# Sixteen pairs in all seven products, rows finished as they complete, stores from a second queue

## The chip, the cores and the metric

One core of a Trainium2 chip runs the kernel. The metric is the device time of one execution in microseconds (us); lower is better. The unchanged kernel has three timed runs and one profiled execution. Engines are named as in the profile: PE (TensorE matmul), DVE (VectorE), ACT (ScalarE), POOL (GpSimd), SP (SyncE); SPq is SP's instruction queue, from which the kernel before issues its DMAs.

## The reference

One residual block on 1024 rows of width 1024, in float32: two attention branches, a gated merge, an output projection and a squared-ReLU MLP of inner width 4096. The change lies in the last two steps and in how their results travel:

```python
merged = gate_sb * (y_sb @ w_sb_out[l]) + gate_diff * (y_diff @ w_diff_out[l])
x = x + rms_norm(merged @ w_o[l], g_post_mix[l])

h = rms_norm(x, g_pre_mlp[l])
u = jnp.square(jax.nn.relu(h @ w_up[l]))
x = x + rms_norm(u @ w_down[l], g_post_mlp[l])
```

`rms_norm(y, g)` divides each row by the root of its mean square and multiplies by `g`.

## The kernel before, in words

Every operand of a matmul is a float32 number split in two: `hi` is a rounded cast (ACT, L607) and `lo` the rest (DVE, L608). A product of two blocks is then three matmuls: hi by hi, hi by lo, lo by hi. A scheduler fixes the order of each engine's instructions ahead of time, from the order of the program and from when buffers come free; on the chip each engine runs its list strictly in order and waits on semaphores. The same is true of SP's list of DMAs. Buffers come from pools with few slots: two for raw loads, four `row` buffers, four wide ones (`wide`), sixteen `big`, twenty-four pages for split operands (`page`, `pair_page`).

**Merge (`finish_tile`, L647 to L688).** For each tile t of 128 rows: the product with `w_o` in two halves, their mean squares on ACT (L666, in the helper at L108), the reciprocal root on POOL (`rstd_of`, L114 to L117), scaling and residual on DVE (L670, L671), a store of the new residual to `x2_dram` (L672), a second mean square (L674), a second norm (L676), eight transposes on PE and, for tiles 0 to 6, a store of the transposed tile to `h_dram` (L688). Tile 7 stays on the chip and is put straight into `hraw` (L684). `load_h` (L707) reads the other tiles back as `hraw`. Between tiles the program loads and splits the first four pairs' blocks of `w_up` (`ahead`, L751) and makes the first pair's weight sums on POOL (`sums0`, L754).

**Up projection (`up_pair`, L816).** The inner width is sixteen pairs n. Each pair is done as a 2x2 block product with seven block products in place of eight (84 matmuls a pair). The products `c` of the first four pairs are begun early (L776 to L787): `p` is a copy of the first product (L783), then PE adds the next product to the same bank. A pair leaves u11, u12, u21, u22 after squared ReLU (ACT, L769 and L770). The first fifteen pairs make sums S1 to S4 of these on POOL (L866 to L869, tiles `us`); the parts and sums are stored to `s_dram` by SP (L874), in order: A11, A12, A22, S1 to S4. Pair 15 stores its four parts and makes no sums.

**Down projection (L883 to L972).** Again seven block products, named by their left factor: A11, S1, S2, A22, S3, S4, A12. The left factor is read back from `s_dram` (`load_a`), the right factor comes from `w_down` (`load_b`, the `b_a`, `b_b`, ... tiles in `row` buffers) or from differences T1 to T4 of its blocks made on POOL (`sub`, L910; the tiles `t`). Each product runs over eight blocks pp of two pairs. For every pp PE does 24 matmuls, six for each of four row tiles, all four open at once in four PSUM banks. As pair 15 is left out, the last pp has 12, and a product 180. At the end of each product its four banks are added to or copied into `lower` and `upper` (L951 to L972), on ACT, DVE and POOL; after S3 POOL does twelve of these (L966 to L968).

**Pair 15 and the finish (L975 to L1014).** After the seven products pair 15 is done plainly: for each of eight row tiles twelve matmuls `dn` (L997), two adds (L1003), the mean square (L1008 at L108), the reciprocal root on POOL, a multiplication by `g_post2` (L1010, on POOL for six tiles, on DVE for two), the residual (L1013, two instructions) and two stores to `out`.

Of the kernel before, what the change touches and what calls it, by code (L numbers as in the profile page):

```python
# [16 lines left out]
P = 128  # L17
# [24 lines left out]
def hybrid_block_kernel(  # L42
# [67 lines left out]
    def rstd_of(ms, pool, name):  # L110
# [25 lines left out]
        for name in ("A11", "A12", "A21", "A22", "S1", "S2", "S3", "S4")  # L136
# [510 lines left out]
    def finish_tile(t):  # L647
# [168 lines left out]
    def up_pair(n):  # L816
# [46 lines left out]
        if n < UP - 1:  # L863
            us12, us34 = wide(f"us12_{n}"), wide(f"us34_{n}")
            s1, s2, s3, s4 = us12[:, 0, :], us12[:, 1, :], us34[:, 0, :], us34[:, 1, :]
            nc.gpsimd.tensor_tensor(s1, u12, u22, op=ALU.add)  # L866
            nc.gpsimd.tensor_tensor(s2, s1, u11, op=ALU.subtract)
            nc.gpsimd.tensor_tensor(s3, u11, u12, op=ALU.subtract)
            nc.gpsimd.tensor_tensor(s4, u21, s2, op=ALU.subtract)  # L869
            parts |= {"S1": s1, "S2": s2, "S3": s3, "S4": s4}  # L870
        else:
            parts["A21"] = u12
        for name, part in parts.items():
            nc.sync.dma_start(out=s_dram[name][n // 2][:, n % 2, :], in_=part)  # L874
# [4 lines left out]
    for n in range(UP):  # L879
        up_pair(n)  # L880


    PP = UP // 2  # L883
    wd = w_down.rearrange("(pp e j p) (k d) -> j k pp p e d", e=2, j=2, p=P, k=2)
    lower, upper, p5s, chain = [], [], [], []

    def entries(pp):
        return 2 if pp < PP - 1 else 1

    def load_a(name, pp):  # L890
        raw = raw_tile(f"{name}_{pp}", [P, 2, HALF])
        n = entries(pp)
        nc.sync.dma_start(out=raw[:, :n, :], in_=s_dram[name][pp][:, :n, :])
        return raw

    def load_b(j, k, pp, name):
        raw = row(f"b{j}{k}_{name}_{pp}", [P, 2, HALF])
        n = entries(pp)
        nc.sync.dma_start(out=raw[:, :n, :], in_=wd[j, k, pp, :, :n, :])
        return raw  # L900

    def parts_of(raw, name, pp):
        n = entries(pp)
        hi, lo = pair_page(f"{name}_hi{pp}"), pair_page(f"{name}_lo{pp}")
        split(hi[:, :n, :], lo[:, :n, :], raw[:, :n, :])
        return hi, lo

    def sub(out, in0, in1, pp):
        n = entries(pp)
        nc.gpsimd.tensor_tensor(out[:, :n, :], in0[:, :n, :], in1[:, :n, :], op=ALU.subtract)  # L910

    def right(name, pp):

        if name == "B11":
# [21 lines left out]

    for left, other in zip(STORED, ("B11", "T1", "T2", "T4", "T3", "B22", "B21")):
        accs = [bank(BANKS[t], f"d{left}_{t}") for t in range(4)]
        for pp in range(PP):
            a_hi, a_lo = parts_of(load_a(left, pp), f"l{left}", pp)  # L940
            b_hi, b_lo = parts_of(right(other, pp), f"r{other}", pp)
            for e in range(entries(pp)):
                for t in range(4):
                    ts = slice(t * P, (t + 1) * P)
                    for i, (st, mv) in enumerate(((a_hi, b_hi), (a_hi, b_lo), (a_lo, b_hi))):
                        nc.tensor.matmul(  # L946
                            accs[t], st[:, e, ts], mv[:, e, :],
                            start=(pp == 0 and e == 0 and i == 0), stop=(pp == PP - 1 and i == 2),
                        )
        for t in range(4):  # L950
            if left == "A11":  # L951
                lower.append(big.tile([P, 2, HALF], F32, tag="big", name=f"lower{t}"))
                nc.scalar.copy(lower[t][:, 0, :], accs[t])
            elif left == "S1":
                if t % 2 == 0:
                    p5s.append(big.tile([P, 2, HALF], F32, tag="big", name=f"p5_{t}"))
                nc.scalar.copy(p5s[t // 2][:, t % 2, :], accs[t])
            elif left == "S2":
                nc.vector.tensor_tensor(lower[t][:, 1, :], accs[t], lower[t][:, 0, :], op=ALU.add)
            elif left == "A22":  # L960
                upper.append(big.tile([P, 2, HALF], F32, tag="big", name=f"upper{t}"))
                nc.scalar.copy(upper[t][:, 0, :], accs[t])
            elif left == "S3":
                v, q, p4, p5 = lower[t][:, 1, :], upper[t][:, 1, :], upper[t][:, 0, :], p5s[t // 2][:, t % 2, :]
                nc.vector.tensor_tensor(q, accs[t], v, op=ALU.add)
                nc.gpsimd.tensor_tensor(p4, q, p4, op=ALU.subtract)  # L966
                nc.gpsimd.tensor_tensor(q, q, p5, op=ALU.add)
                nc.gpsimd.tensor_tensor(v, v, p5, op=ALU.add)  # L968
            elif left == "S4":
                nc.vector.tensor_tensor(lower[t][:, 1, :], accs[t], lower[t][:, 1, :], op=ALU.add)  # L970
            else:
                nc.vector.tensor_tensor(lower[t][:, 0, :], accs[t], lower[t][:, 0, :], op=ALU.add)  # L972


    g_post2 = load_row(2, big.tile([P, D], F32, tag="big", name="grow2"))  # L975
    last_a, last_b = [], []
    for j in range(2):
        raw = raw_tile(f"last_a{j}", [P, 2, HALF])
        for i in range(2):
            nc.sync.dma_start(out=raw[:, i, :], in_=s_dram[f"A{i + 1}{j + 1}"][PP - 1][:, 1, :])  # L980
        parts = pair_page(f"last_a_hi{j}"), pair_page(f"last_a_lo{j}")
        split(*parts, raw)
        last_a.append(parts)
        raw = row(f"last_b{j}", [P, 2, HALF])
        f = NF - 2 + j
        nc.sync.dma_start(out=raw, in_=w_down[f * P:(f + 1) * P, :].rearrange("p (k d) -> p k d", k=2))
        parts = pair_page(f"last_b_hi{j}"), pair_page(f"last_b_lo{j}")
        split(*parts, raw)
        last_b.append(parts)
    for i, t in enumerate((4, 5, 6, 7, 0, 1, 2, 3)):  # L990
        c, ts = t // 4, slice((t % 4) * P, (t % 4 + 1) * P)
        accs = [bank(BANKS[(2 * i + n) % 4], f"dn_{t}_{n}") for n in range(2)]
        for j in range(2):
            (a_hi, a_lo), (b_hi, b_lo) = last_a[j], last_b[j]
            for p, (st, mv) in enumerate(((a_hi, b_hi), (a_hi, b_lo), (a_lo, b_hi))):
                for n in range(2):
                    nc.tensor.matmul(  # L997
                        accs[n], st[:, c, ts], mv[:, n, :],
                        start=(j == 0 and p == 0), stop=(j == 1 and p == 2),
                    )  # L1000
        tot = (upper if c else lower)[t % 4]
        for n in range(2):
            nc.vector.tensor_tensor(tot[:, n, :], accs[n], tot[:, n, :], op=ALU.add)  # L1003
        tot = tot.rearrange("p a b -> p (a b)")
        xt, o = row(f"xf_{t}"), row(f"of_{t}")
        nc.sync.dma_start(out=xt, in_=x2_dram[t * P:(t + 1) * P, :])
        s2 = pb.tile([P, 1], F32, tag="ssq1", name=f"sf2_{t}", bufs=4)
        mean_square(tot, o, s2)  # L1008
        r = rstd_of([s2], pb, f"f{t}")
        (nc.vector if i > 5 else nc.gpsimd).tensor_tensor(tot, tot, g_post2, op=ALU.mult)  # L1010
        for n in range(2):
            ns = slice(n * HALF, (n + 1) * HALF)
            nc.vector.scalar_tensor_tensor(o[:, ns], tot[:, ns], r, xt[:, ns], op0=ALU.mult, op1=ALU.add)  # L1013
# [51 lines left out]
```

## Time and profile before

| what | value |
|---|---|
| median of three runs | 1494.95 us (1494.24 to 1495.29) |
| profiled execution, its own time | 1494.08 us |
| its span | 1492.4 us |
| outside the span | 1.68 us |
| PE busy | 1443.9 us, 97% of the span |
| DVE, ACT, POOL busy | 64%, 50%, 28% |
| DMA | 217.88 MB, 146 GB/s on average |

The span runs from the first to the last instruction of the profiled execution. PE's busy time is modelled per matmul with overlap, so the time of a run of matmuls is read from their starts. Where this text says cadence, it means the distance between the starts of two matmuls that follow each other.

### The profile page before, as it was taken

The page shows a single profiled execution, that of the slowest core. Times are in us where ns is not written, and L with a number is a line of the kernel's source. Part 1 is how long each engine was busy: PE and PEld are TensorE (multiplying, and loading weights), DVE is VectorE, ACT ScalarE, POOL GpSimd, SP SyncE. Part 2 cuts the span into 40 slices and gives each one's busy share as a digit, 9 for nine tenths or more (in the row PEclk, how much of TensorE's full clock was granted, in tenths as well). Part 3 has the DMA queues.
Part 4 walks back from the last instruction along what each step waited for, and adds up shares of the span by engine and source line. Part 5 has one row for each costly group of instructions (what it writes and reads, how often), then busy time and mean ns, then how long its engine had stood idle before and what let it go on. Part 6 is the DMA issues. An engine that isn't in the chain of part 4 may idle for free. (4 is left out here: it accounts for less than half of the span.)

```text
span 1492.4 us, 20173 instructions
## 1 busy us (share of the span) xinstructions
PE 1443.9 (97%) x7314; PEld 1224.5 (82%) x7314; DVE 955.7 (64%) x1410; ACT 739.4 (50%) x1338; POOL 414.4 (28%) x378
## 2 busy tenths in 40 slices
PE   7999999999999999999999898999999999999993
PEld 6888998898889888888888676887888888888883
DVE  5487988898688857545644675444445598646536
ACT  6456766676465555743334453444444345344312
POOL 2022322230000000000011247656665463334206
PEclk9999999999999999999999999999999999999997
DMA  5342213222332253644356734444446775677615
GB/s 201 81 126 64 71 43 85 71 61 64 85 89 82 78 170 128 212 137 152 102 193 206 269 113 148 162 145 158 158 153 233 246 241 171 209 246 243 202 43 197
DMA packets 93867, 217.88 MB, mean 146 GB/s; under 512 B 9308, under 2 KB 25928, under 8 KB 93768
## 3 DMA queue, kind: packets, MB, share of 16 engines
q1 hardware_dynamic: 93768, 216.61, 44.8%
q8 instruction: 57, 0.93, 0.3%
q14 instruction: 42, 0.34, 0.1%
HBM read 150.75 MB, written 59.79 MB: 141 GB/s over the span
## 5 line engine op out<-in xcount | busy, mean ns | idle before, releaser
L198 PE MATMUL acc_gate<-h_hi,lo_gate 128*128 128x512 f32 x256 | 101.0, 394 | 0.0
L196 PE MATMUL acc_gate<-h_hi,hi_gate 128*128 128x512 f32 x256 | 100.8, 394 | 0.0
L331 DVE TENSOR_TENSOR_SCAN rest<-rest 128x896 f32<-128x896 f32 (+3 forms) x64 | 87.6, 1373 | 20.7 <-POOL rest L326 20.3
L197 PE MATMUL acc_gate<-h_lo,hi_gate 128*128 128x512 f32 x256 | 100.7, 393 | 0.0
L326 POOL TENSOR_SCALAR_AFFINE_SELECT rest<-rest 128x128 f32<-128x128 f32 x64 | 23.6, 369 | 240.3 <-ACT rest L322 223.6
L608 DVE TENSOR_TENSOR w_lo<-raw_up,w_hi 128x1024 fp32r<-128x1024 f32 x32 | 44.4, 1397 | 49.8 <-ACT w_hi L607 43.3
L608 DVE TENSOR_TENSOR lS_lo<-raw_S,lS_hi 128x1024 fp32r<-128x1024 f32 (+1 forms) x32 | 49.3, 1540 | 37.4 <-ACT lS_hi L607 37.3
L607 ACT CAST lS_hi<-raw_S 128x1024 fp32r<-128x1024 f32 (+1 forms) x32 | 32.0, 1000 | 80.8 <-DMA raw_S<-s_dramS 46.8
L116 POOL TENSOR_SCALAR rstd_o<-s 128x1 f32<-128x1 f32 x8 | 2.8, 356 | 244.7 <-DVE or L670 212.8
L946 PE MATMUL dS<-rT_hi,lS_hi 128*128 128x512 f32 x180 | 70.0, 389 | 0.0
L946 PE MATMUL dS<-rT_lo,lS_hi 128*128 128x512 f32 x180 | 70.0, 389 | 0.0
L946 PE MATMUL dS<-rT_hi,lS_lo 128*128 128x512 f32 x180 | 70.0, 389 | 0.0
L567 PE MATMUL mix<-y,hi_mix 128*128 128x512 f32 x256 | 68.6, 389 | 0.0
L394 ACT ACTIVATE s<-s,low 128x896 f32<-128x896 f32 (+7 forms) x64 | 49.7, 777 | 28.3 <-DVE low L389 28.0
L375 POOL MEMSET bias<- 64x64 f32 x4 | 0.6, 144 | 214.0 <-DMA bias<-bias_rows 154.1
L389 DVE CUSTOM_DVE_ANT_0 s<-z,bias 128x512 f32<-128x512 f32 (+3 forms) x64 | 37.0, 586 | 32.0 <-PE z L263 26.7
L608 DVE TENSOR_TENSOR lA_lo<-raw_A,lA_hi 128x1024 fp32r<-128x1024 f32 (+1 forms) x24 | 38.2, 1593 | 28.7 <-ACT lA_hi L607 24.7
L763 PE MATMUL c<-hB_hi,wa_hi 128*128 128x512 f32 x128 | 51.0, 398 | 5.5 <-ACT p L783 5.5
L567 PEld LDWEIGHTS mix<-y,hi_mix 128*128 128x128 f32 x256 | 48.0, 188 | 9.9
L198 PEld LDWEIGHTS acc_gate<-h_hi,lo_gate 128*128 128x128 f32 x256 | 48.1, 188 | 9.2
L197 PEld LDWEIGHTS acc_gate<-h_lo,hi_gate 128*128 128x128 f32 x256 | 48.2, 188 | 8.8
L196 PEld LDWEIGHTS acc_gate<-h_hi,hi_gate 128*128 128x128 f32 x256 | 48.2, 188 | 8.6
(352 smaller groups left out, 4860.7 us busy)
## 6 DMA issues: line engine op xcount, KB each, us to landing
raw_up<-in_w_up_dram SPq DMA_DIRECT2D x32, 512.0 KB, 4.2
s_dramS<-us SPq DMA_DIRECT2D x60, 256.0 KB, 2.4
raw_S<-s_dramS SPq DMA_DIRECT2D x28, 512.0 KB, 4.2
s_dramA<-u SPq DMA_DIRECT2D x49, 256.0 KB, 2.7
raw_A<-s_dramA SPq DMA_DIRECT2D x21, 512.0 KB, 3.7
raw_gate<-in_w_in_dram SPq DMA_DIRECT2D x16, 512.0 KB, 3.7
gate_dram<-gt SPq DMA_DIRECT2D x32, 256.0 KB, 2.5
y<-y_dram SPq DMA_DIRECT2D x16, 512.0 KB, 6.6
```

The costliest lines, as they stand in the source:

```text
L196: nc.tensor.matmul(acc, w_hi[:, ks], h_hi[k][:, cs], start=(k == 0), stop=False)
L197: nc.tensor.matmul(acc, w_hi[:, ks], h_lo[k][:, cs], start=False, stop=False)
L198: nc.tensor.matmul(acc, w_lo[:, ks], h_hi[k][:, cs], start=False, stop=(k == NK - 1))
L326: nc.gpsimd.affine_select(tl[:, dg], tl[:, dg], pattern=[[-1, P]], compare_op=ALU.is_gt, fill=fill, base=0, channel_multiplier=1,)
L331: nc.vector.tensor_tensor_scan(back, back, back, 1.0, op0=ALU.mult, op1=ALU.bypass)
L389: nc.vector.tensor_tensor_reduce(out=s[:, c0:c1], in0=z, in1=bias[:, S - nk + c0:S - nk + c1], scale=1.0, scalar=BIG if prev is None else ...
L394: e = nc.scalar.activation(s[:, :nk], s[:, :nk], AF.Exp, bias=low, scale=-1.0, accum_out=sums[:, m:m + 1],)
L567: nc.tensor.matmul(accs[i][c], st[:, ks], mv[:, cs], start=(first and k % 4 == 0), stop=(last and k % 4 == 3),)
L607: nc.scalar.copy(hi, raw)
L608: nc.vector.tensor_tensor(lo, raw, f32(hi), op=ALU.subtract)
L763: nc.tensor.matmul(acc, st[:, ks], mv, start=(first and k == 0 and i == 0), stop=(k == 3 and i == 2), skip_group_check=True,)
L946: nc.tensor.matmul(accs[t], st[:, e, ts], mv[:, e, :], start=(pp == 0 and e == 0 and i == 0), stop=(pp == PP - 1 and i == 2),)
```

## The change

- All sixteen pairs go through the seven products. `up_pair` makes S1 to S4 for pair 15 too; `A21` is no longer stored, `entries` and the plain `dn` stage are gone. A product has 192 matmuls.
- Rows are finished when their last product is: tiles 4 to 7 after S3; of tiles 0 to 3 the second half's mean square and gain after S4, the first half and the rest after A12. The mean square is taken by halves, the gain is applied by DVE in halves of 512, and `rstd_of` adds two sums. The last four pp of A12 (`BY_TILE`) are done row tile by row tile, so that the tiles end one after the other.
- ACT issues the stores to `x2_dram` (after the mean square), to `h_dram`, and those of A11, A12 and A22. SP keeps S1 to S4, the output and all loads.
- The `ahead` weights are loaded and split after tile 0, not tile 3; `sums0` comes after tile 4, not tile 5; the first two B11 blocks of `w_down` (`first_b`) are loaded ahead of pair 15.

```diff
-        nc.sync.dma_start(out=x2_dram[t * P:(t + 1) * P, :], in_=xt)
         ssq = pb.tile([P, 1], F32, tag="ssq1", name=f"sx_{t}", bufs=4)
         mean_square(xt, o, ssq)
+        nc.scalar.dma_start(out=x2_dram[t * P:(t + 1) * P, :], in_=xt)
...
-            nc.sync.dma_start(out=h_dram[j][c][:, :, ts], in_=ht.rearrange("p (k t) -> p k t", k=4))
+            nc.scalar.dma_start(out=h_dram[j][c][:, :, ts], in_=ht.rearrange("p (k t) -> p k t", k=4))
...
         finish_tile(t)
+        if t == 0:
+            for n in range(AHEAD):
+                first_a.append(split_f0(n, raw_up(2 * n, f"ahead{n}")))
...
-            for n in range(AHEAD):
-                first_a.append(split_f0(n, raw_up(2 * n, f"ahead{n}")))
-        if t == 5:
+        if t == 4:
             sums0 = sums(0, stream.tile([P, HALF], F32, tag="tmp", name="s1_0", bufs=1))
...
-        if n < UP - 1:
...
+        parts |= {"S1": s1, "S2": s2, "S3": s3, "S4": s4}
         for name, part in parts.items():
-            nc.sync.dma_start(out=s_dram[name][n // 2][:, n % 2, :], in_=part)
+            queue = nc.sync if name[0] == "S" else nc.scalar
+            queue.dma_start(out=s_dram[name][n // 2][:, n % 2, :], in_=part)
...
-            b11, b12 = load_b(0, 0, pp, "a"), load_b(0, 1, pp, "a")
+            b11, b12 = first_b[pp] if pp < 2 else load_b(0, 0, pp, "a"), load_b(0, 1, pp, "a")
...
+    for n in range(UP - 1):
+        up_pair(n)
+    first_b = [load_b(0, 0, pp, "a") for pp in range(2)]
+    up_pair(UP - 1)
...
+    def begin_rows(t, tot):
+        xt, o = big_f32(f"xf_{t}"), big_f32(f"of_{t}")
+        nc.sync.dma_start(out=xt.rearrange("p a b -> p (a b)"), in_=x2_dram[t * P:(t + 1) * P, :])
+        s2 = pb.tile([P, 2], F32, tag="ssq", name=f"sf2_{t}", bufs=4)
+        pending[t] = tot, xt, o, s2
+
+    def half_rows(t, n):
+
+        tot, xt, o, s2 = pending[t]
+        mean_square(tot[:, n, :], o[:, n, :], s2[:, n:n + 1])
+        nc.vector.tensor_tensor(tot[:, n, :], tot[:, n, :], g_post2[:, n * HALF:(n + 1) * HALF], op=ALU.mult)
+
+    def end_rows(t):
+        tot, xt, o, s2 = pending[t]
+        r = rstd_of([s2[:, 0:1], s2[:, 1:2]], pb, f"f{t}")
+        for n in range(2):
+            nc.vector.scalar_tensor_tensor(o[:, n, :], tot[:, n, :], r, xt[:, n, :], op0=ALU.mult, op1=ALU.add)
+            nc.sync.dma_start(out=out[t * P:(t + 1) * P, n * HALF:(n + 1) * HALF], in_=o[:, n, :])
...
+            begin_rows(4 + t, upper[t])
+            for n in range(2):
+                half_rows(4 + t, n)
+            end_rows(4 + t)
...
+            half_rows(t, 0)
+            end_rows(t)
...
+        together = PP - BY_TILE if left == "A12" else PP
+        kept = []
         for pp in range(PP):
...
+            factors = parts_of(load_a(left, pp), f"l{left}", pp), parts_of(right(other, pp), f"r{other}", pp)
+            if pp >= together:
+                kept.append(factors)
+                continue
+            for t in range(4):
+                accumulate(accs[t], factors, t, pp == 0, pp == PP - 1)
         for t in range(4):
+            for i, factors in enumerate(kept):
+                accumulate(accs[t], factors, t, False, i == len(kept) - 1)
+            evict(left, t, accs[t])
```

The scheduler puts the new instructions into the engines' lists. The following pieces show three places; the numbers behind the names are buffer numbers.

POOL at the passage from the up to the down projection, before (`us` are the sums S1 to S4, `t` the differences of blocks of `w_down`):

```order
L866 TENSOR_TENSOR us_14_11142<-u_14_11035,u_14_11036 128x512
L868 TENSOR_TENSOR us_14_11143<-u_14_11035 128x512
L867 TENSOR_TENSOR us_14_11142<-us_14_11142,u_14_11035 128x512
L869 TENSOR_TENSOR us_14_11143<-u_14_11036,us_14_11142 128x512
L910 TENSOR_TENSOR t_0_11304<-b_a_11302,b_a_11300 128x1024
L910 TENSOR_TENSOR t_1_11344<-b_a_11342,b_a_11340 128x1024
```

The same place in the change:

```order
L869 TENSOR_TENSOR us_14_11135<-u_14_11028,us_14_11134 128x512
L866 TENSOR_TENSOR us_15_11282<-u_15_11175,u_15_11176 128x512
L868 TENSOR_TENSOR us_15_11283<-u_15_11175 128x512
L867 TENSOR_TENSOR us_15_11282<-us_15_11282,u_15_11175 128x512
L869 TENSOR_TENSOR us_15_11283<-u_15_11176,us_15_11282 128x512
L900 TENSOR_TENSOR t_0_11309<-b_a_11307,b_a_11147 128x1024
L900 TENSOR_TENSOR t_1_11347<-b_a_11345,b_a_11149 128x1024
```

Pair 15's four sums now stand ahead of the first difference `t_0`.

SP at the same passage, before (`b_a` are the loads of `w_down` for the first product; 11380 and 11382 belong to pp 2):

```order
L874 DMA s_dramS_155<-us_14_11143 128x512
L893 DMA raw_A_4_11454<-s_dramA_96 128x1024
L874 DMA s_dramA_123<-u_15_11180 128x512
L874 DMA s_dramA_99<-u_15_11179 128x512
L899 DMA b_a_11380<-in_w_down_dram 128x2x512
L899 DMA b_a_11382<-in_w_down_dram 128x2x512
```

In the change (11383 and 11385 belong to pp 2):

```order
L873 DMA s_dramS_147<-us_14_11135 128x512
L886 DMA raw_A_4_11457<-s_dramA_96 128x1024
L873 DMA s_dramS_123<-us_15_11282 128x512
L873 DMA s_dramS_139<-us_15_11283 128x512
L873 DMA s_dramS_131<-us_15_11282 128x512
L873 DMA s_dramS_147<-us_15_11283 128x512
L891 DMA b_a_11383<-in_w_down_dram 128x2x512
L891 DMA b_a_11385<-in_w_down_dram 128x2x512
```

The loads for pp 2 now stand behind the four stores of pair 15's sums; before, two stores of pair 15's parts stood there.

ACT where the merge ends and the first products `c` of the up projection begin, before:

```order
L687 COPY ht_1_8830<-trh_1_8825 128x512
L108 ACTIVATE or_8900,s_7_8902<-o_0_8833 128x512
L108 ACTIVATE or_8900,s_7_8902<-o_1_8834 128x512
L783 COPY p_0_8932<-c_0_8936 128x512
L108 ACTIVATE or_8900,sx_8912<-xr_8899 128x1024
L783 COPY p_0_8932<-c_1_8937 128x512
```

In the change:

```order
L687 COPY ht_1_8822<-trh_1_8817 128x512
L108 ACTIVATE or_8892,s_7_8894<-o_0_8825 128x512
L108 ACTIVATE or_8892,s_7_8894<-o_1_8826 128x512
L688 DMA h_dram_89<-ht_0_8814 512x1x128
L688 DMA h_dram_91<-ht_1_8822 512x1x128
L108 ACTIVATE or_8892,sx_8903<-xr_8891 128x1024
L674 DMA x_dram<-xr_8891 128x1024
L784 COPY p_0_8924<-c_0_8928 128x512
L784 COPY p_0_8924<-c_1_8929 128x512
```

The two stores of the transposed tile 6 and the store of tile 7's residual stand in ACT's list, and both copies `p` stand behind tile 7's second mean square, where before one of them stood ahead of it.

## Rows read from the trace of the kernel before

**Rows 1.** The page, part 1: busy time and share of the span by engine.
```profile
PE 1443.9 (97%) x7314; PEld 1224.5 (82%) x7314; DVE 955.7 (64%) x1410; ACT 739.4 (50%) x1338; POOL 414.4 (28%) x378
```

**Rows 2.** The chain of waits: start us, length us, what, number of instructions.
```profile
849.54 5.29 PE c L763 x12
...
1203.12 81.60 PE dS L946 x360
...
1447.92 7.95 PE dn L997 x35
```

**Rows 3.** Timeline of the end: start, length, engine, line, operation, [idle before <- releaser].
```profile
1469.07 0.61 PE L997 MATMUL dn<-last_b_hi,last_a_lo 128*128 128x512 f32 x2
...
1487.87 1.42 DVE L1013 SCALAR_TENSOR_TENSOR of<-lower,rstd_f,xf 128x512 f32<-128x512 f32 x2 [0.76 <-POOL rstd_f L117]
```

**Rows 4.** Windows: stretch, length; busy of PE, PEld, DVE, ACT, POOL; PEclk; DMA share; GB/s.
```profile
840.00:860.00 20.00, 14.51 (x58) 11.54 (x58) 13.46 (x17) 8.25 (x17) 7.35 (x8) 0.83 0.65 218
...
1460.00:1480.00 20.00, 9.68 (x43) 7.70 (x41) 11.96 (x19) 4.60 (x8) 13.29 (x13) 0.81 0.76 244
1480.00:1492.00 12.00, 0.00 (x0) 0.00 (x0) 6.60 (x8) 2.30 (x4) 4.51 (x6) 0.50 0.56 206
```

**Rows 5.** Timeline, merge: two half stores of `h_dram`, and one tile's norm by halves.
```profile
785.22 1.20 SPq L688 DMA_DIRECT2D h_dram<-ht  x2
...
787.41 0.59 ACT L108 ACTIVATE or<-o 128x512 f32<-128x512 f32 x1
...
789.18 1.28 DVE L671 SCALAR_TENSOR_TENSOR xr<-or,rstd_o,xr 128x1024 f32<-128x1024 f32 x1 [0.34 <-POOL rstd_o L117]
```

**Rows 6.** Timeline, passage from up to down: loads and casts of pp 2, pair 15's ends.
```profile
1159.23 1.97 SPq L899 DMA_DIRECT2D b_a<-in_w_down_dram  x4
...
1162.19 0.69 DVE L856 TENSOR_TENSOR u<-p_av,v 128x512 f32<-128x512 f32 x1 [5.93 <-issue]
...
1162.61 0.39 PE L763 MATMUL p_tr<-hT_hi,w_lo 128*128 128x512 f32 x1
...
1162.95 1.05 ACT L607 CAST rB_hi<-b_a 128x1024 fp32r<-128x1024 f32 x1 [4.16 <-DMA b_a<-in_w_down_dram]
1163.04 0.69 DVE L859 TENSOR_TENSOR u<-p_tr,v 128x512 f32<-128x512 f32 x1 [0.16 <-PE p_tr L763]
...
1163.90 0.63 ACT L769 ACTIVATE u<-u 128x512 f32<-128x512 f32 x1
...
1173.04 0.39 PE L946 MATMUL dA<-rB_hi,lA_hi 128*128 128x512 f32 x1
```

**Rows 7.** Timeline, same passage: POOL instructions and DVE splits beside them and alone.
```profile
1148.05 1.31 POOL L868 TENSOR_TENSOR us<-u 128x512 f32<-128x512 f32 x1
...
1168.25 1.23 DVE L608 TENSOR_TENSOR rB_lo<-b_a,rB_hi 128x1024 fp32r<-128x1024 f32 x1 [1.52 <-ACT rB_hi L607]
...
1169.32 2.41 POOL L910 TENSOR_TENSOR t<-b_a,b_a 128x1024 f32<-128x1024 f32 x1 [9.03 <-DMA s_dramA<-u]
1169.73 3.08 DVE L608 TENSOR_TENSOR lA_lo<-raw_A,lA_hi 128x1024 fp32r<-128x1024 f32 x1 [0.25 <-ACT lA_hi L607]
```

**Rows 8.** Groups by line, 1180 to 1445 us, POOL: busy, mean ns, idle before.
```profile
L910 POOL TENSOR_TENSOR b_c<-t,b_c 128x1024 f32<-128x1024 f32 (+1 forms) x8 | 22.1, 2763 | 33.3 <-DMA b_c<-in_w_down_dram 33.2
...
L966 POOL TENSOR_TENSOR upper<-upper 128x512 f32<-128x512 f32 x4 | 8.4, 2110 | 24.4 <-DVE upper L965 24.4
L967 POOL TENSOR_TENSOR upper<-upper,p 128x512 f32<-128x512 f32 x4 | 8.0, 2034 | 0.0
L968 POOL TENSOR_TENSOR lower<-lower,p 128x512 f32<-128x512 f32 x4 | 7.7, 1914 | 0.0
```

**Rows 9.** Timeline where the merge ends: DVE's residual of tile 7, PE's next `c`.
```profile
845.56 2.27 DVE L671 SCALAR_TENSOR_TENSOR xr<-or,rstd_o,xr 128x1024 f32<-128x1024 f32 x1 [7.75 <-POOL rstd_o L117]
...
849.54 0.80 PE L763 MATMUL c<-hB_hi,wa_hi 128*128 128x512 f32 x1 [5.49 <-ACT p L783]
```

**Rows 10.** Waits of SP's DMA queue: us in total, times, longest.
```profile
SPq L874 <- ACT u L770: 130.4, 43, 9.4
```

More of the change, by code (lines that the diff above doesn't have):

```diff
@@ L135, in hybrid_block_kernel @@
         name: [dram.tile([P, 2, HALF], F32, name=f"s_dram{name}{i}") for i in range(NF // 4)]
-        for name in ("A11", "A12", "A21", "A22", "S1", "S2", "S3", "S4")
+        for name in ("A11", "A12", "A22", "S1", "S2", "S3", "S4")
     }
@@ L862, in up_pair @@
         parts = {"A11": u11, "A12": u21, "A22": u22}
-        if n < UP - 1:
[L864 to L872, printed above, removed]
+        us12, us34 = wide(f"us12_{n}"), wide(f"us34_{n}")
+        s1, s2, s3, s4 = us12[:, 0, :], us12[:, 1, :], us34[:, 0, :], us34[:, 1, :]
+        nc.gpsimd.tensor_tensor(s1, u12, u22, op=ALU.add)
+        nc.gpsimd.tensor_tensor(s2, s1, u11, op=ALU.subtract)
+        nc.gpsimd.tensor_tensor(s3, u11, u12, op=ALU.subtract)
+        nc.gpsimd.tensor_tensor(s4, u21, s2, op=ALU.subtract)
+        parts |= {"S1": s1, "S2": s2, "S3": s3, "S4": s4}
         for name, part in parts.items():
-            nc.sync.dma_start(out=s_dram[name][n // 2][:, n % 2, :], in_=part)
+            queue = nc.sync if name[0] == "S" else nc.scalar
+            queue.dma_start(out=s_dram[name][n // 2][:, n % 2, :], in_=part)
     def tmp1(name):
         return stream.tile([P, HALF], F32, tag="tmp", name=name, bufs=1)
-    for n in range(UP):
-        up_pair(n)
     PP = UP // 2
+    BY_TILE = 4
     wd = w_down.rearrange("(pp e j p) (k d) -> j k pp p e d", e=2, j=2, p=P, k=2)
     lower, upper, p5s, chain = [], [], [], []
-    def entries(pp):
-        return 2 if pp < PP - 1 else 1
     def load_a(name, pp):
         raw = raw_tile(f"{name}_{pp}", [P, 2, HALF])
-        n = entries(pp)
-        nc.sync.dma_start(out=raw[:, :n, :], in_=s_dram[name][pp][:, :n, :])
+        nc.sync.dma_start(out=raw, in_=s_dram[name][pp])
         return raw
@@ L922, in right @@
         if name == "T2":
-            sub(chain[pp], load_b(1, 1, pp, "b"), chain[pp], pp)
+            sub(chain[pp], load_b(1, 1, pp, "b"), chain[pp])
             return chain[pp]
@@ L926, in right @@
             b21 = load_b(1, 0, pp, "c")
-            sub(b21, chain[pp], b21, pp)
+            sub(b21, chain[pp], b21)
             return b21
@@ L930, in right @@
             b22, b12 = load_b(1, 1, pp, "d"), load_b(0, 1, pp, "d")
-            sub(b12, b22, b12, pp)
+            sub(b12, b22, b12)
             return b12
@@ L935, in right, with accumulate @@
         return load_b(1, 0, pp, "f")
+    def accumulate(acc, factors, t, first, last):
+        (a_hi, a_lo), (b_hi, b_lo) = factors
+        ts = slice(t * P, (t + 1) * P)
+        for e in range(2):
+            for i, (st, mv) in enumerate(((a_hi, b_hi), (a_hi, b_lo), (a_lo, b_hi))):
+                nc.tensor.matmul(
+                    acc, st[:, e, ts], mv[:, e, :], start=(first and e == 0 and i == 0), stop=(last and e == 1 and i == 2)
+                )
+    for n in range(UP - 1):
+        up_pair(n)
@@ new lines, in end_rows, with evict @@
+    def end_rows(t):
[4 more added lines that the diff above has]
+            nc.sync.dma_start(out=out[t * P:(t + 1) * P, n * HALF:(n + 1) * HALF], in_=o[:, n, :])
+    def evict(left, t, acc):
+        if left == "A11":
+            lower.append(big_f32(f"lower{t}"))
+            nc.scalar.copy(lower[t][:, 0, :], acc)
+        elif left == "S1":
+            if t % 2 == 0:
+                p5s.append(big_f32(f"p5_{t}"))
+            nc.scalar.copy(p5s[t // 2][:, t % 2, :], acc)
+        elif left == "S2":
+            nc.vector.tensor_tensor(lower[t][:, 1, :], acc, lower[t][:, 0, :], op=ALU.add)
+        elif left == "A22":
+            upper.append(big_f32(f"upper{t}"))
+            nc.scalar.copy(upper[t][:, 0, :], acc)
+        elif left == "S3":
+            v, q, p4, p5 = lower[t][:, 1, :], upper[t][:, 1, :], upper[t][:, 0, :], p5s[t // 2][:, t % 2, :]
+            nc.vector.tensor_tensor(q, acc, v, op=ALU.add)
+            nc.gpsimd.tensor_tensor(p4, q, p4, op=ALU.subtract)
+            nc.gpsimd.tensor_tensor(q, q, p5, op=ALU.add)
+            nc.gpsimd.tensor_tensor(v, v, p5, op=ALU.add)
+            begin_rows(4 + t, upper[t])
+            for n in range(2):
+                half_rows(4 + t, n)
+            end_rows(4 + t)
+        elif left == "S4":
+            nc.vector.tensor_tensor(lower[t][:, 1, :], acc, lower[t][:, 1, :], op=ALU.add)
+            begin_rows(t, lower[t])
+            half_rows(t, 1)
+        else:
+            nc.vector.tensor_tensor(lower[t][:, 0, :], acc, lower[t][:, 0, :], op=ALU.add)
+            half_rows(t, 0)
+            end_rows(t)
@@ L937, in hybrid_block_kernel @@
     for left, other in zip(STORED, ("B11", "T1", "T2", "T4", "T3", "B22", "B21")):
         accs = [bank(BANKS[t], f"d{left}_{t}") for t in range(4)]
+        together = PP - BY_TILE if left == "A12" else PP
+        kept = []
         for pp in range(PP):
[L940 to L949, printed above, removed]
@@ L950, in hybrid_block_kernel @@
-        for t in range(4):
[L951 to L972, printed above, removed]
@@ L975, in hybrid_block_kernel @@
[L975 to L989, printed above, removed]
@@ L990, in hybrid_block_kernel @@
[L990 to L1013, printed above, removed]
-            nc.sync.dma_start(out=out[t * P:(t + 1) * P, ns], in_=o[:, ns])
```

19 lines of the change are left out of this document (10 added, 9 removed).

## The prediction

> **What bounds the kernel now.** The page's first part comes first: PE is busy 97% of the span [rows 1], so the question is where PE stands still, and what it is given to do. The chain of waits says the same: from 1163 us on it is PE alone, 360 matmuls in 81.60 us [rows 2], a cadence of 226.7 ns, 2.72 us for 12. The reader should see that no load and no split is on the chain there. The windows show two holes. From 1480 us PE does nothing to the end, and in 840 to 860 it is busy 14.51 of 20 us, at a mean granted clock of 0.83 [rows 4]. The end is read from its timeline: the row at 1469.07 holds two `dn` matmuls, so the last starts at about 1469.3; DVE's last two instructions run from 1487.87 to 1489.29 and the span ends at 1492.4 [rows 3]. That is a tail of 23.1 us in which rows queue up behind POOL's norms and gains.
>
> **The sum,** against the profiled execution's own 1494.08 us.
>
> 1. *Matmuls.* Before, 7 x 180 + 96 = 1356; now 7 x 192 = 1344. Twelve fewer at 226.7 ns: **-2.7 us**, all on the chain.
>
> 2. *The tail.* Rows 4 to 7 are done while S4 and A12 still run, and A12's row tiles end 24 matmuls apart, 5.44 us. After the last matmul one row tile is left, of which one half is new: from the last matmul's start to DVE's add 0.43 us (the last `p_tr` at 1162.61, the add L859 at 1163.04 [rows 6]); the add 0.69 [rows 6]; a start of 0.1; from the start of the half's mean square on ACT through the accumulator read and both POOL instructions to DVE's next instruction 1.77 (787.41 to 789.18 [rows 5]), in which DVE's gain for the half, about as long as the add, is hidden; both residual instructions 1.42, and 3.1 from their end to the end of the span [rows 3]. Sum 7.5 us. The tiles do not queue: add, norm and residual are 4 us, less than the 5.44 between tiles. 7.5 in place of 23.1: **-15.6 us.**
>
> 3. *The passage to the down projection.* Here the change adds a wait. Before, the four `b_a` loads of pp 2 and 3 left SP from 1159.23 and pp 2's cast began at 1162.95, 3.72 us later; PE came to pp 2 at 1173.04 [rows 6], so there were ten microseconds in hand. Now POOL has pair 15's four sums ahead of `t_0`, `t_0` must free a `row` buffer before pp 2 can be loaded, and SP has the four stores of those sums ahead of that load. Step by step: u12 is added at 1162.19 to 1162.88 [rows 6]; two ACT instructions of 0.63 [rows 6] give it squared at 1164.2; four POOL sums at 1.31 [rows 7], 1169.5; `t_0` 2.41 [rows 7], 1171.9; issue and landing 3.72 [rows 6], 1175.7; the cast 1.05 [rows 6], 1176.8; the split's `lo`, which the second matmul needs, 1.23 alone or 3.08 beside a POOL difference [rows 7], so 1178.0 to 1179.9. The second matmul was due at 1173.3: PE waits 4.7 to 6.6 us. I take 5.6, the middle, because POOL's `t_2` becomes ready within a microsecond of that split and either may go first. **+5.6 us.** Later pp don't add to it: POOL needs 2.41 per difference, PE 5.44 per pp.
>
>    The row at 1169.73 shows DVE's split at 3.08 us beside POOL's difference, and 1.23 alone [rows 7]. The Trainium skill, page "SBUF — State Buffer", section "SBUF: two separate sides", has a rule for such a pair: a DVE instruction with both inputs in SBUF and a GpSimd instruction that reads SBUF exclude each other for a whole instruction. By that rule the split would wait out `t_2` and the wait would be 6.6, making the sum one microsecond worse; the rows agree with the rule where they overlap, but don't say which of the two starts first.
>
> 4. *The clock after that wait.* After PE's idle 5.49 us at 849.54 [rows 9], the next 12 matmuls took 5.29 in place of 2.72 [rows 2], at half the usual rate, and the window's granted clock was 0.83 [rows 4]; of the two levels 1.2 and 2.4 GHz that is the lower one for a while. A wait of about the same length should cost the same: **+2.6 us**; bounds 0 and 2.6.
>
> 5. *The end of the merge.* Before, PE lost 5.5 us because ACT's second copy `p` stood behind tile 7's second mean square, which waited for DVE's residual at 845.56, 7.75 us late [rows 9]. Now both copies stand behind it, so PE runs dry 12 matmuls earlier, 2.7 us; against that the `ahead` casts and splits no longer sit between tiles 4 and 7, and their loads don't share the queues with those of `sums0`. But `sums0`, one tile earlier, stands ahead of tile 6's norm on POOL and waits for its loads, and ACT has the stores of `h_dram` in its list, which `hraw` waits for. I find terms of up to 4 us in both directions and none that stands out: **0**, bounds -4 and +4.
>
> 6. *Stores from ACT.* SP waited 130.4 us in 43 pieces for ACT's squares before it could store them [rows 10], with loads queued behind. Now 70 stores are issued by ACT. Before shows no DMA issued by ACT; on SP the two `h_dram` stores took 1.20 us together [rows 5], so at most 0.6 each, some 40 us in all, of which ACT, busy 50% [rows 1], hides most. Where it is wanted is the merge, and that price is within point 5. From 860 to 1160 PE is paced by POOL or itself, so neither price nor gain: 0, with -2 as the bound of a gain. The rows would let one expect much more from freeing SP. The Trainium skill, page "DMA: Bandwidth & Descriptors", section "Issuing engines are not separate DMA queues", speaks against that: transfers started from several engines share the same 16 DMA engines, and only issue time is saved. By it no transfer gets shorter and this point stays 0; no row of before can test it.
>
> 7. *The finish of rows 4 to 7.* POOL's twelve instructions after S3 are as before, 24.1 us [rows 8], and the norm of row 4 now stands behind them. DVE, in order, waits there for about 26 us after S3's end, with the split of S4's last pp and of A12's first behind. S4's last pp is due 7 x 5.44 = 38 us after S3's end, A12's first 43.5; DVE gets to them at about 28 and 34. Covered by some 9 us: **0.** SP's loads for A12's third pp stand behind rows 4 to 6 in the same way, due at 54.
>
> Sum: -2.7 - 15.6 + 5.6 + 2.6 = -10.1, so 1484.0 for the profiled execution; it ran 0.87 below the median of the runs, hence **1484.9 us**.
>
> **The rivals.**
>
> *The passage costs nothing (chance 0.17).* If the scheduler's waits let pp 2's load go before `t_0` is done, or pair 15's squares come sooner, points 3 and 4 drop out: 1484.9 - 8.2 = 1476.7. For it: PE has ten microseconds in hand there. Against: POOL's list has nothing else to do first.
>
> *The merge gains (0.12) or loses (0.13)* its 4 us: 1481 or 1489. For a loss: both `p` copies behind the late mean square. For a gain: DMA and ACT are freed of the `ahead` weights where tile 6 was late.
>
> *Slower: DVE starves the tail products (0.04).* One mechanism: POOL's twelve instructions and DVE's splits take turns, DVE waits for row 4's norm, and A12's first split comes after A12 is due. Its price is nothing until the norm is 9 us late; that takes POOL instructions of 2.8 us instead of 2.0. At 4.2 each, 50 us in all, A12 would stand 17 us and lose 2.6 more at the low clock: 1484.9 + 20 = 1505. From about 3.5 us each it is slower than before. Against: the same twelve took 1.9 to 2.1 beside splits in before, and even twice as wide ones take 2.8 [rows 8].
>
> *The tail is not shortened (0.04).* If a row tile's finish waited for another engine, say the x2 load or POOL, each end would take over 5.44 us and pile up to ten more: about 1494, the same as before.
>
> The forecast has the remaining 0.5.
>
> **How the numbers follow.** Between forecast and rivals the bounds are: below, no wait at the passage and a gain of 2, 1475; above, a wait of 6.6, the clock's 2.6 and the merge's 4 with ACT's issues, 1491. Range **1475 to 1491**; some 0.1 lies on either side. A measurement of this kernel can tell about 0.2%, 3 us, from no change. Faster by more than that: forecast, first two rivals: 0.91. Within: the unshortened tail and part of the merge's loss: 0.05. Slower: 0.04.
>
> **What would show it.** Right: no `dn` rows; PE idle once at about 1173 for 5 to 6 us before the 49th `dA` matmul, put down to ACT's cast or DVE's `lo` of `b_a`, with a dozen matmuls at twice the cadence after it; the last matmul about 7.5 us before the span's end; PE without idle from S1 to the end. The merge's step is wrong if PE's loss in 840 to 930 differs by over 4 us. The forecast as a whole is wrong if PE idles in S4 or A12, or if the tail after the last matmul is over 10 us.

## The result, and the profile after

The change takes the median from 1494.6 us (four runs of the kernel before on that chip) to 1483.11 us (1482.16 to 1485.69): a ratio of 0.993, 95% interval 0.9911 to 0.9948. The forecast was 1484.9. The profiled execution ran 1482.92 us; its span went from 1492.4 to 1481.2.

First the chain of waits after the change, the passage to the down projection and the products (start us, length us, what):

```profile
1169.68 2.41 POOL t L900
...
1172.10 3.89 DMA b_a<-in_w_down_dram
...
1176.02 1.05 ACT rB_hi L607
...
1177.11 35.30 PE dA L935 x144
1212.42 87.04 PE dS L935 x384
...
1430.02 43.53 PE dA L935 x192
```

These rows answer to [rows 2]. 384 matmuls take 87.04 us, the cadence of before, 226.7 ns, and `dn` is gone. At the passage the chain leaves PE for POOL's `t`, a load and a cast, as it didn't before. The 144 matmuls behind it take 35.30 us in place of 32.64 (144 at 226.7 ns): 2.7 us at a lower clock, granted at 0.50 in 1176 to 1182 us.

The passage in its timeline, POOL, SP, ACT and DVE, then PE's first matmuls of pp 2:

```profile
1164.57 1.29 POOL L866 TENSOR_TENSOR us<-u,u 128x512 f32<-128x512 f32 x1 [11.68 <-ACT u L771]
...
1165.89 4.18 SPq L873 DMA_DIRECT2D s_dramS<-us  x4
...
1168.43 1.29 POOL L869 TENSOR_TENSOR us<-u,us 128x512 f32<-128x512 f32 x1
...
1172.10 3.21 SPq L891 DMA_DIRECT2D b_a<-in_w_down_dram  x4
...
1177.09 1.23 DVE L608 TENSOR_TENSOR rB_lo<-b_a,rB_hi 128x1024 fp32r<-128x1024 f32 x1 [13.14 <-ACT rB_hi L607]
...
1177.49 3.06 POOL L900 TENSOR_TENSOR t<-b_a,b_a 128x1024 f32<-128x1024 f32 x1 [3.09 <-DMA b_a<-in_w_down_dram]
```

```profile
1177.11 2.08 PE L935 MATMUL dA<-rB_hi,lA_hi 128*128 128x512 f32 x4 [3.69 <-ACT rB_hi L607]
```

The reader sees the steps of the forecast in order, each within 0.4 us of the time worked out for it, and PE idle for 3.69 us. The load leaves at 1172.10, just as `t` (1169.68, 2.41 long) has ended; the four stores of the sums are out two microseconds earlier. Before, the cast for pp 2 stood at 1162.95 [rows 6].

The end, in the timeline of PE and of the others:

```profile
1473.15 0.39 PE L935 MATMUL dA<-rB_hi,lA_lo 128*128 128x512 f32 x1
```

```profile
1473.57 0.69 DVE L995 TENSOR_TENSOR lower<-dA,lower 128x512 f32<-128x512 f32 x1 [1.00 <-PE dA L935]
1474.30 0.63 ACT L108 ACTIVATE of<-lower 128x512 f32<-128x512 f32 x1 [4.71 <-DVE lower L995]
...
1475.05 0.69 DVE L958 TENSOR_TENSOR lower<-lower,grow 128x512 f32<-128x512 f32 x1 [0.79 <-ACT of L108]
1475.12 0.79 POOL L116 TENSOR_SCALAR rstd_f<-sf 128x1 f32<-128x1 f32 x1 [4.00 <-ACT of L108]
...
1476.59 1.41 DVE L964 SCALAR_TENSOR_TENSOR of<-lower,rstd_f,xf 128x512 f32<-128x512 f32 x2 [0.84 <-POOL rstd_f L117]
```

One row tile's chain is all that is left: 8.05 us from the last matmul's start to the span's end at 1481.2, where [rows 3] had 23.1.

PE's waits from 830 to 1165 us (us in total, times, longest):

```profile
PE c L764 <- ACT u L770: 4.1, 2, 2.5
PE p_sc L764 <- ACT w_hi L607: 3.9, 3, 1.6
PE p_sc L764 <- DVE w_lo L608: 2.2, 3, 1.0
PE c L764 <- DVE or L670: 2.2, 1, 2.2
PE p_av L764 <- DVE u L852: 1.8, 1, 1.8
PE c L764 <- ACT p L846: 1.3, 1, 1.3
```

The 5.49 us wait for the copy `p` [rows 9] is gone, and smaller ones have come: for DVE's scaling of tile 7 (L670), for ACT's squares of the first `u` (L770), for copies in the up stage. PE does the merge's last matmul at 833.1 us (835.5 before) and the up stage's last at 1162.8 (1162.6 before). Of these 2.4 us, 0.7 lie ahead of the merge, where the kernels are the same, and 1.7 in the merge; all of it is lost again in the up stage.

So the 11.2 us of span are: 2.7 for twelve matmuls, 15.1 for the tail, less 6.4 for the passage and its clock, less 0.2 up to there. That is one profiled execution of each kernel.

### The profile page after: what moved, and what is told of

Read it like the earlier page. It is cut to its first block, busy times and chain, and to the rows that moved or that the text cites. A ratio compares the mean times of both kernels' runs of the same rounds, so it can differ in the third digit from the quotient of the medians.

```text
span 1481.2 us, 20077 instructions
## 1 busy us (share of the span) xinstructions
PE 1442.6 (97%) x7302; PEld 1222.0 (83%) x7302; DVE 959.9 (65%) x1404; ACT 742.8 (50%) x1350; POOL 406.4 (27%) x376
## 4 chain that ended last, share of the span: by engine, by line
PE 80%; issue 7%; POOL 5%; DVE 3%; DMA 2%; ACT 1%; SPq 0%; POOLq 0%; DVEq 0%; ACTq 0%
PE dS L935 12%; PE dA L935 8%; PE o L656 6%; PE mix L567 6%; PE acc_gate L198 4%; PE acc_gate L196 4%; PE acc_gate L197 4%; PE c L764 3%; PE p_av L764 3%; PE p_tr L764 3%; PE z L263 2%; PE z L262 2%; PE tr_sb L281 2%; PE p_sc L764 1%; PE tr_df L281 1%
## 5 line engine op out<-in xcount | busy, mean ns | idle before, releaser
L608 DVE TENSOR_TENSOR lS_lo<-raw_S,lS_hi 128x1024 fp32r<-128x1024 f32 x32 | 59.7, 1866 | 38.5 <-ACT lS_hi L607 38.3
L935 PE MATMUL dS<-rT_hi,lS_hi 128*128 128x512 f32 x192 | 74.7, 389 | 0.0
L935 PE MATMUL dS<-rT_lo,lS_hi 128*128 128x512 f32 x192 | 74.7, 389 | 0.0
L935 PE MATMUL dS<-rT_hi,lS_lo 128*128 128x512 f32 x192 | 74.7, 389 | 0.0
L607 ACT CAST lS_hi<-raw_S 128x1024 fp32r<-128x1024 f32 x32 | 33.7, 1052 | 78.5 <-DMA raw_S<-s_dramS 50.0
L116 POOL TENSOR_SCALAR rstd_o<-s 128x1 f32<-128x1 f32 x8 | 2.4, 299 | 239.7 <-DVE wa_lo L608 212.2
L726 POOL TENSOR_TENSOR s<-raw_up 128x512 f32<-128x512 f32 x16 | 24.4, 1527 | 117.2 <-DMA raw_up<-in_w_up_dram 87.5
L770 ACT ACTIVATE u<-u 128x512 f32<-128x512 f32 x48 | 29.6, 628 | 51.9 <-DVE u L852 24.5
```

The costliest lines, as they stand in the source:

```text
L608: nc.vector.tensor_tensor(lo, raw, f32(hi), op=ALU.subtract)
L935: nc.tensor.matmul(acc, st[:, e, ts], mv[:, e, :], start=(first and e == 0 and i == 0), stop=(last and e == 1 and i == 2))
```

## The experiments

All are edits of the changed kernel. Ratios are to the kernel before on the same chip. Four chips were used, on which its median was 1493.91 to 1494.10 us, so the medians are compared directly.

| run | median us | ratio, 95% interval |
|---|---|---|
| the changed kernel again | 1484.79 | 0.9944 (0.9932 to 0.9956) |
| sums late | 1479.12 | 0.9901 (0.9887 to 0.9916) |
| all stores on SP | 1479.52 | 0.9901 (0.9889 to 0.9914) |
| weights late | 1481.93 | 0.9919 (0.9906 to 0.9932) |
| stores on SP and weights late | 1483.46 | 0.9933 (0.992 to 0.9945) |
| rows on SP, parts on ACT | 1481.15 | 0.9912 (0.9898 to 0.9925) |
| parts on SP, rows on ACT | 1484.75 | 0.9929 (0.9917 to 0.9941) |
| sums late, all stores on SP | 1472.61 | 0.9855 (0.984 to 0.987) |
| sums late, only parts on ACT | 1476.69 | 0.988 (0.9867 to 0.9894) |
| sums late, only rows on ACT | 1477.76 | 0.9887 (0.9871 to 0.9903) |
| A12 not by tile | 1488.27 | 0.996 (0.9946 to 0.9974) |
| gain of rows 4 to 7 on POOL | 1485.43 | 0.9943 (0.9928 to 0.9958) |

**The yardstick.** The changed kernel without an edit.

> The changed kernel once more, on the same chip as the three others, as their yardstick. Both theories: 1483 us, within 2 us.

1484.79 us, in line. It shows how far one profiled execution can be trusted: the work ahead of the merge, the same in all these kernels, did its last matmul between 740.3 and 742.8 us. The yardstick's own profiled execution took 1488.16 us, and its up projection, from the merge's last matmul to the up stage's last, took 333.4 us, where it had taken 329.8 in the first profile of the same kernel.

**The passage.** Pair 15's sums behind `t_0` and `t_1`, in other buffers:

```diff
+        if n == UP - 1:
+            store(n, parts)
+            late.append((u11, u12, u21, u22))
+        else:
+            store(n, parts | sums_of(n, u11, u12, u21, u22, wide))
...
+    LATE_AT = 1
...
+            if left == "A11" and pp == LATE_AT:
+                store(UP - 1, sums_of(UP - 1, *late[0], pair_f32))
```

> Pair 15's four sums are put behind the first two differences t_0 and t_1 on POOL, and their stores behind the loads of pp 2 and 3 on SP; they live in pages, so that t_0 and t_1 can have the wide buffers of pair 14. Nothing else moves. Theory (the passage wait comes from t_0 and the pp 2 load standing behind the sums): the wait of 3.7 us and the dozen matmuls at the lower clock (2.7 us more) both go, PE runs 384 + 192 matmuls in one piece from 1163 us, and the time falls by 6.4 us to about 1476.7. Rival (the wait only moves: t_2 now stands behind the sums, and pp 4 is late): PE idles at about 1184 in place of 1173 and the gain is under 3 us.

1479.12 us, 5.7 less than the yardstick. In its chain of waits the first product runs through at full rate, and no wait comes in its place:

```profile
1165.60 42.84 PE dA L947 x189
1208.44 87.04 PE dS L947 x384
```

From the up stage's last matmul to the very last it takes 304.0 us, the changed kernel 310.3: the 6.4 us forecast for this run. The cause of the wait is settled, and so is that the slow dozen came with it. The run moves the sums and their stores together; that the load waited for POOL, not for the stores, is read from the timeline above.

**Who issues the stores.** All back on SP:

```diff
-        nc.scalar.dma_start(out=x2_dram[t * P:(t + 1) * P, :], in_=xt)
+        nc.sync.dma_start(out=x2_dram[t * P:(t + 1) * P, :], in_=xt)
-            nc.scalar.dma_start(out=h_dram[j][c][:, :, ts], in_=ht.rearrange("p (k t) -> p k t", k=4))
+            nc.sync.dma_start(out=h_dram[j][c][:, :, ts], in_=ht.rearrange("p (k t) -> p k t", k=4))
-            queue = nc.sync if name[0] == "S" else nc.scalar
+            queue = nc.sync
```

> All stores go back to SP's queue; x2_dram's stays behind the mean square in the program. Theory (who issues the stores is worth nothing, since PE in the up stage waits for POOL and for itself): 1483 within 2 us. Rival (SP's 130 us of waits for ACT's squares held loads back, and freeing SP is a part of the gain): 3 us or more slower than the changed kernel, PE waits in 860 to 1160 us grown by that.

1479.52 us: both theories fell. Stores on SP are neither the same nor slower, but 3.6 to 5.3 us faster than the changed kernel's (1483.11 and 1484.79). Why SP gained nothing from losing them is read from its waits; no run moves the stores of S1 to S4 as well. After the change, over the whole span:

```profile
SPq L873 <- POOL us L866: 128.2, 16, 12.1
```

Before it waited 130.4 us for ACT's squares [rows 10]. The sums S1 to S4 are still in its list, and the first of them waits for POOL, which waits for the same squares. The place of the wait moved by one instruction; the loads behind it gained nothing. POOL's wait for the loads of `w_up`, 880 to 1165 us, stayed too: 82.9 us in 13 pieces before, and after the change

```profile
POOL s L726 <- DMA raw_up<-in_w_up_dram: 86.9, 13, 9.0
```

**The weights.** `ahead` after tile 3 and `sums0` after tile 5 again, once with ACT's stores and once with SP's:

```diff
-        if t == 0:
-            for n in range(AHEAD):
-                first_a.append(split_f0(n, raw_up(2 * n, f"ahead{n}")))
...
+            for n in range(AHEAD):
+                first_a.append(split_f0(n, raw_up(2 * n, f"ahead{n}")))
-        if t == 4:
+        if t == 5:
```

> The ahead weights are loaded after tile 3 again and the first sums after tile 5; all else as in the change. Theory (the merge's gains and losses cancel, PE enters the down projection 0.2 us later than before the change): 1483 within 3 us. Rival (the earlier weights gain several us which the ACT-issued stores give back): 1486 or more, with PE idle in 840 to 860 us as long as before the change or longer.

> Stores on SP and the weights at their former places: of the change, sixteen pairs and the new finish are left, with the early first_b. Theory (the early weights bring PE out of the merge 2 us sooner, and this is kept where SP issues the stores): 2 us above the run with all stores on SP, 1481 to 1482. Rival (early weights are worth nothing or harm, as the run with late weights at 1481.9 beside 1484.8 says): 1479.5 or less.

1481.93 and 1483.46 us. With SP's stores the early weights gain 3.9 us (1483.46 to 1479.52); with ACT's they gain nothing (1481.93 late; 1483.11 and 1484.79 early). The first is as its theory had it, the second 1.5 us above its theory and not near its rival. The profiles put a part of the gain in the merge: from its first matmul to its last it takes 92.2 us in nine of the eleven profiles with early weights, and 94.7 with SP's stores and late weights (93.9 before). PE's waits from 830 to 880 us show more of it: with SP's stores and late weights the old wait is there,

```profile
PE c L763 <- ACT p L783: 4.9, 1, 4.9
```

with early weights it is shorter (1.6 to 3.0 in the four profiles with early weights and the rows' stores on SP),

```profile
PE c L764 <- ACT p L784: 3.0, 2, 2.8
```

and in the changed kernel, rows given above, ACT's squares and DVE's scaling cost 6.3 us in its place. The run with SP's stores and late weights has a use of its own. Sixteen pairs, the new finish, the early loads of two `w_down` blocks and the later store to `x2_dram` are what it keeps of the change, and it gains 10.5 us, near points 1 to 4 of the forecast, -10.1; its passage waits 3.6 us and its tail is 8.0. What the last two are worth no run separates.

**Rows or parts.** Only `x2_dram` and `h_dram` on SP (the first two of the three edits that put all stores there), or only A11, A12, A22 (the third):

```diff
-            queue = nc.sync if name[0] == "S" else nc.scalar
+            queue = nc.sync
```

> Only the stores of x2_dram and h_dram go back to SP; the parts A11, A12, A22 stay with ACT. Theory (the parts, 48 issues among the squares and copies of the up stage, are what costs): like the changed kernel, 1483 to 1485. Rival (the merge's 22 stores cost it, since hraw waits for h_dram): like all stores on SP, about 1479.5.

> Only the parts A11, A12, A22 go back to SP; x2_dram and h_dram stay with ACT. Theory: like all stores on SP, about 1479.5, with PE's idle time between 1000 and 1070 us small. Rival (the merge's stores cost it): 1483 to 1485.

1481.15 and 1484.75 us. The theory that the parts cost it fell: here the rows' stores, 22 in all, cost 5.2 us over SP's and the parts 1.6. The 1.6 is not clear of noise, and the five runs with the rows on ACT lay between 1480.46 and 1485.22 us.

**Together.** Sums late and all stores on SP, by the edits above, and then each kind of store given back to ACT:

> The sums behind the first differences, as in the run of the late sums, and all stores on SP, as in the run with SP's stores. Theory (the two are independent: the passage's 6.4 us, and some 4 us of PE's idle time in the up stage that comes with ACT-issued stores): 1473 to 1475, PE enters the down projection at about 1160.4 us and takes 304 us for it. Rival (the passage with SP-issued parts has its own late load, since parts and sums stand in one queue): 1477 or more, with PE idle behind 1170.

> Sums behind the first differences, x2_dram and h_dram stored by SP, only the parts A11, A12, A22 by ACT: the best version so far (1472.6 us) with the parts' 48 issues on ACT. Theory (the parts' issuer shifts PE's idle time within the up stage but hardly its sum): 1472 to 1475. Rival (each issue on ACT delays squares that POOL waits for): 1476 or more.

> Sums behind the first differences, parts stored by SP, only x2_dram and h_dram by ACT. Theory (the rows' stores in ACT's list hold up tile 7's squares and the first u, with PE waiting 2.2 us for DVE's L670 and 3 us for ACT's L770, and cost 2 to 5 us): 1475 to 1478. Rival (the 1484.75 us of the earlier run with rows on ACT came from elsewhere, its spread was 1480.5 to 1485.2): 1472.6 to 1474.

1472.61, 1476.69 and 1477.76 us, the last as its theory had it. The two gains add up (5.7 and 5.3, together 12.2 below the yardstick), and the first of the three is the best version: 1.45% below the kernel before, and some 10 to 12 us below the change. On top of it the parts on ACT cost 4.1 us, against the theory, and the rows 5.2; both together cost 6.5 (1479.12), less than their sum.

Where the costs arise is shown less surely. The up projection took 325.8 us with all on SP, 329.2 with the parts on ACT, 328.3 with the rows, 331.9 with both, but the same changed kernel had 329.8 and 333.4. Of the 4.7 and 4.4 us between these profiled executions, 1.9 and 2.6 lie ahead of the merge, where the kernels are the same.

The waits are steadier. For the rows the place is the first `c` products; PE's waits from 830 to 1165 us with the rows on ACT:

```profile
PE c L764 <- ACT u L770: 2.8, 2, 2.5
...
PE c L764 <- DVE or L670: 2.2, 1, 2.2
```

and with all on SP, where none is for these squares:

```profile
PE c L764 <- ACT p L784: 1.6, 2, 1.4
...
PE c L764 <- DVE or L670: 0.6, 1, 0.6
```

That is 2.8 us of the rows' 5.2. With early weights, all seven profiles with the rows on ACT wait 2.2 us for L670 and at least 2.7 for L770, and the four with the rows on SP wait 0.6 for L670 and not for L770. For the parts the loss shows between 1000 and 1070 us, as waits for a copy `p` (L846, 1.4) and a sum `u` (L852, 1.8; 0.9 with all on SP), with slow matmuls behind them: the granted clock was 0.89 in 1020 to 1035 us, and 1.00 with all on SP. With early weights the wait for this `p` is 1.1 to 1.8 us in all seven profiles with the parts on ACT, and 0.3 or none with the parts on SP. What sets these waits is the order that comes out for ACT, DVE and SP together, and no run separates it.

**The finish.** A12's tiles ended together:

```diff
-    BY_TILE = 4
+    BY_TILE = 0
```

> BY_TILE is 0: A12's four row tiles run together to the end, as the other products do, so they end 0.7 us apart and not 5.44; all else as in the change. Theory (the tail is one row tile's chain only because the tiles end far apart; DVE needs 0.69 + 0.69 + 1.42 = 2.8 us for each): three more tiles queue on DVE, the tail after the last matmul is 8.1 + 3 x 2.8 - 3 x 0.7 = 14 us, and the time some 6 us more, 1489 to 1491. Rival (the tail got shorter because rows 4 to 7 are gone from it and one half is done early; spacing is worth little): a tail under 10 us and 1483 to 1486.

1488.27 us, 3.5 to 5.2 more. The last matmul and the last residual in its timeline, span 1487.9:

```profile
1476.85 0.39 PE L935 MATMUL dA<-rB_hi,lA_lo 128*128 128x512 f32 x1
```

```profile
1483.28 1.41 DVE L964 SCALAR_TENSOR_TENSOR of<-lower,rstd_f,xf 128x512 f32<-128x512 f32 x2 [0.46 <-POOL rstd_f L117]
```

The tail is 11.05 us, between the two theories. So 3 of the 15 us are due to the spacing, since DVE fills gaps of one tile with another's work: from 1475.78 to 1482.83 us it goes without a break from one row tile's add, gain or residual to another's. The other 12 are put down to what is finished earlier by subtraction, not by a run.

**The slack of rows 4 to 7.** Their gain on POOL:

```diff
-        nc.vector.tensor_tensor(tot[:, n, :], tot[:, n, :], g_post2[:, n * HALF:(n + 1) * HALF], op=ALU.mult)
+        (nc.gpsimd if t > 3 else nc.vector).tensor_tensor(tot[:, n, :], tot[:, n, :], g_post2[:, n * HALF:(n + 1) * HALF], op=ALU.mult)
```

> The gain of rows 4 to 7, eight instructions of 128x512, goes from DVE to POOL, between and behind its twelve instructions after S3; all else as in the change. In the change DVE split A12's first pp some 14 us ahead of need. Theory (that slack covers the norms of rows 4 to 7 on POOL, and is what a slower finish there eats first): POOL's part grows by 14 to 18 us, A12's first split comes about when it is due, PE idles 0 to 4 us ahead of A12, and the time is 0 to 7 us more. Rival (DVE's order doesn't hold A12 back at all): A12's first split stays 10 us or more ahead, no idle PE, 1483 to 1485.

1485.43 us, and no idle PE. DVE waits 8.45 us for row 4's norm, and still splits A12's first pp at once:

```profile
1413.76 2.45 DVE L964 SCALAR_TENSOR_TENSOR of<-upper,rstd_f,xf 128x512 f32<-128x512 f32 x2 [8.45 <-POOL rstd_f L117]
1416.13 2.31 DVE L608 TENSOR_TENSOR lA_lo<-raw_A,lA_hi 128x1024 fp32r<-128x1024 f32 x1
1418.37 2.32 DVE L608 TENSOR_TENSOR rB_lo<-b_f,rB_hi 128x1024 fp32r<-128x1024 f32 x1
```

```profile
1433.24 43.53 PE dA L935 x192
```

It is ready 12.6 us ahead of need, as in the changed kernel (12.8). The theory took DVE's list as fixed; the scheduler put the split ahead of row 5's finish. The last row tile's norm, some 11 us later against S3's end, held nothing up.

## Why the prediction was right

It was right in sign, size and, for the most part, place; that the stores and early weights came to nothing in the sum was luck.

*Point 1* (-2.7) stands in the chain: 1344 matmuls at the same cadence.

*Point 2* (-15.6) measured -15.1. Each step held but one: from ACT's mean square to DVE's residual it took 2.29 us, not 1.77, because POOL's L116 took 0.79 here. It runs beside DVE's gain and ends just after it, 1475.91 and 1475.74. The Trainium skill, page "SBUF — State Buffer", section "SBUF: two separate sides", says that a DVE instruction with two inputs in SBUF and a GpSimd instruction that reads SBUF exclude each other; the trace agrees, even for a POOL instruction of 128x1, 0.30 us long where nothing is beside it.

*Point 3* (+5.6) was oversized: 3.7, below the 5 to 6 us named as its sign. Its chain came out as worked out. What failed is the step from the split to PE: I let the second matmul wait for `lo`, and let POOL's `t_2` delay the split. The split started 0.4 us ahead of `t_2`, and PE's list had four hi by hi matmuls of pp 2 at its head, so that `lo` was not missed. I had read POOL's and SP's lists there, and not PE's.

*Point 4* (+2.6) measured 2.7, and without the wait it is not there.

*Points 5 and 6* (0) came out as a sum, +0.2 us to the up stage's end, and were wrong in their parts, so the hit is luck. In the yardstick's profile, of an execution of 1488.16 us, PE left the up stage at 1168.3 us, 5.7 later than before. Point 5's own test, that PE's loss in 840 to 930 us should not change by over 4, came out at the bound in one profile and well inside it in the other: PE did 322 matmuls there before and 340 in the changed kernel, 4.1 us less lost at 226.7 ns each, but 318 in the yardstick.

Early weights gain 3.9 us where SP issues the stores; that is the gain I had bounded at 4 without choosing it. The step that failed is point 6: "neither price nor gain". ACT's issues cost 3.6 to 5.3 us in the change as it stands and 6.5 beside late sums (1472.61 to 1479.12). The rows' share of it, as far as the waits show it, lies at the merge's end, whose price point 6 had left to point 5; the parts' share, 4.1 us beside late sums, lies in the stretch that it had put at nothing.

What the Trainium skill states on the page "DMA: Bandwidth & Descriptors", section "Issuing engines are not separate DMA queues", that issuing from several engines saves issue time and no transfer time, agrees with the runs as far as they go: from issue to landing a part's store took 2.6 us (median) from either engine, an `h_dram` store 3.0, and no gain from SP's saving shows. But no price had been put on a place in ACT's list, where the stores of `h_dram`, tile 7's squares and the first `u` stand one behind the other.

*Point 7* (0) held with more to spare than the 9 us given: 12.8, and 12.6 when POOL was given eight instructions more.

Of the rivals none came about. The first, a passage without cost, was made by moving the sums, and is worth 5.7 us where the forecast had 8.2. The slower one is far off: A12's first split was early, not late.

Left open: what in the up stage makes the parts' stores on ACT cost 4.1 us in one pair of kernels and 1.6 in another. In the first pair the granted clock in 1020 to 1035 us fell to 0.89 with the parts on ACT, in the second it stayed at 1.00; but the changed kernel's own two profiles have 0.89 and 1.00 there too.

## What to carry to other kernels

When work is added to a stage's end, read in every engine's list what it now stands ahead of: here four small sums on an idle engine cost 6.4 us, because the next stage's first buffer was freed behind them, and with them two instructions later the wait was gone. Moving DMA issues to a second engine did not free the first one's queue here: stores that waited for the same squares, by way of POOL, stayed in it and kept it as late as it was, and the new queue's own work paid for the issues. A change whose parts cancel shows as nothing in the sum, so test them one by one.

## What the runs showed of the hardware that was not expected

After an idle of 3.3 to 3.8 us in a full stream of matmuls, seen at the passage in nine of these profiled executions, nine to thirteen of the matmuls behind it started over 0.3 us apart in place of 0.23, most of them 0.43: about half rate, the lower of the two levels. In the five where no further wait followed, that cost 1.9 to 3.0 us. In the kernel before, a wait of 5.49 us had cost 2.6. So the shorter wait had about the same price. And POOL's addition of two numbers a row, 0.30 us in the changed kernel's merge, took 0.79 us beside DVE's multiplication of 128x512.
